# Loading x from two queues, and the modulation of the first two channel tiles summed by TensorE from the raw weights

## The chip, the cores and the metric

The kernel runs on one core of one Trainium2 chip. The metric is the device time of one execution in microseconds (us); the time of a version is the median over its runs. TensorE multiplies matrices, VectorE and ScalarE work elementwise, GpSimd does a few small operations, and SyncE issues nearly all DMAs. ScalarE issues some small ones.

## The reference, cut to what matters

One layer of a streaming encoder on `x` (512 x 1024) with a conditioning vector `c` (1024). What matters here is its beginning:

```python
cond = silu(c)
mod = cond @ w_ada + b_ada                 # w_ada: 1024 x 6144
sh1, sc1, g1, sh2, sc2, g2 = split(mod, 6)
u = layer_norm(x) * (1 + sc1) + sh1        # shift and scale per channel
z = u @ w_in                               # 1024 x 8192
```

Then two mixers (a gated recurrence and a spatial gating), their projections, a merge, `w_out`, a layer norm with `g1`, and a SwiGLU feed-forward layer with `sh2`, `sc2` and `g2`. All is in 32-bit floats.

## The kernel before

Channels lie on the partitions in eight tiles of 128 (`k` = 0 to 7), the 512 rows of x in the free dimension. To keep precision, each operand of a large product is split into a high part in a rounded format (`whi`, `uh`) and the rest (`wlo`, `ul`), and three products are summed: `whi*uh`, `wlo*uh`, `whi*ul`.

The part that the change touches is the head, the first 58 us. There:

- `x` comes in four row tiles (`load_x`), all on SyncE's queue. VectorE and GpSimd take each one's statistics, ScalarE normalises it (`x_norm`, L319), and TensorE transposes it channel tile by channel tile (`x_transpose`, L408).
- The small parameters come by ScalarE's queue: `c` into `cond`, and four pieces into the rows of `prow` (L282 to L285). TensorE's first instruction transposes `prow` (L451); ScalarE and GpSimd then make `bmod` from it, the bias of the modulation.
- `ada_cols(k, ...)` makes shift and scale for the two channel tiles k and k+1. It loads 1024 rows of `w_ada` for 256 shift and 256 scale columns in four DMAs of 512 KB. `step(d)` adds row tile d, weighted by `cond`, into the accumulator `adaacc` on VectorE (L346, L344); ScalarE can take a step (L342, into `prod`). `fin` sums the accumulator over the partitions: TensorE multiplies it with a matrix of ones (L363), and VectorE adds the bias (L365).
- `modulate(k)` (L412 to L414) applies shift and scale to the transposed tile: ScalarE makes `uf` and `uh`, VectorE `ul`.
- `lead(k, w, half)` (L420 to L423) multiplies channel tile k with the first 768 columns of the `u` section of `w_in`, in two halves of three column tiles, nine matmuls each. The six accumulators stay in PSUM over all eight channel tiles.
- `warm(n)` issues n products of ones (L401), each of which is two instructions in the profile, as is every 32-bit product here that isn't in the rounded format.

On TensorE, VectorE, ScalarE, GpSimd and SyncE this part runs in the order in which the code is written (`manual_schedule`). In the loop `for p in range(KT // 2)`, each turn has four `lead` calls, two `x_transpose` calls and one `fin`; VectorE works on the sums for the next two channel tiles (`steps`), on `split_part` of the next weight block, and on `modulate`. After the head, everything follows in one long stream on TensorE to the end.

Of the kernel before, what the change touches and what calls it, by code (L numbers as in the profile page):

```python
# [7 lines left out]
F32 = mybir.dt.float32  # L8
# [3 lines left out]
OP = mybir.AluOpType  # L12
# [3 lines left out]
P = 128  # L16
T = 512
NT = T // P
D = 1024
# [12 lines left out]
def f32(ap):  # L32
    return ap.bitcast(F32)
# [17 lines left out]
def body(ctx, tc, x, c, w_ada, b_ada, w_in, b_gate, lb_logits, norm_w, w_proj_a, g_ln_w, g_ln_b,  # L51
         g_ws, g_bs, w_proj_b, w_out, ln1_w, ln1_b, w_ffn_in, w_ffn_out, ln2_w, ln2_b, out):
    nc = tc.nc
    x, out = x[0], out[0]
    w_ada, b_ada, w_in, b_gate, norm_w = w_ada[0], b_ada[0], w_in[0], b_gate[0], norm_w[0]
# [4 lines left out]
    V, A, G, PE = nc.vector, nc.scalar, nc.gpsimd, nc.tensor  # L60
# [5 lines left out]
    ua = ctx.enter_context(tc.tile_pool(name="ua", bufs=12))  # L66
# [8 lines left out]
    def acc_ps():  # L75
        return acc.tile([P, 512], F32, name="acc")

    def side_ps():
        return side.tile([P, 512], F32, name="sps")

    def s2(name="s2"):
        return tmp["s2"].tile([P, 512], F32, name=name, tag="s2")
# [117 lines left out]
    blocks = []  # L200
# [59 lines left out]
    ident = cst.tile([P, P], F32, name="ident")  # L260
# [6 lines left out]
    mhalf = cst.tile([P, 4], F32, name="mhalf")  # L267
    V.memset(mhalf, -0.5)
    cond = cst.tile([P, 8], F32, name="cond")
    nc.scalar.dma_start(cond, c[0].rearrange("(a p) -> p a", p=P))  # L270
    A.activation(cond, cond, AF.Silu)
    par = cst.tile([P, P], F32, name="par")
    bmod = cst.tile([P, 8, 2], F32, name="bmod")
    bmod2 = cst.tile([P, 8, 2], F32, name="bmod2")
    mod1 = cst.tile([P, 8, 2], F32, name="mod1")
# [7 lines left out]
    nc.scalar.dma_start(prow[R_BG:R_BG + 16, :], b_gate.rearrange("g (a b) -> (g a) b", b=P))  # L283
    nc.scalar.dma_start(prow[R_LB:R_LB + 16, :], lb_logits.rearrange("g (a b) -> (g a) b", b=P))
    nc.scalar.dma_start(prow[R_NW:R_NW + 1, :], norm_w.rearrange("(a b) -> a b", b=P))  # L285
    xt = [ua.tile([P, 2, D], F32, name=f"x{i}", tag="u") for i in range(2)]

    def xtile(tt):
        return xt[tt // 2][:, tt % 2, :]

    def load_x(tts):
        for tt in tts:
            nc.sync.dma_start(xtile(tt), x[tt * P:(tt + 1) * P, :])

    load_x((0, 1))


    def ln_stats(xa):
        st = sm.tile([P, 2, 6], F32, name="bst")
# [18 lines left out]
    def normalise(dst, src, rn):  # L318
        A.activation(dst, src, AF.Identity, bias=rn[:, 1:2], scale=rn[:, 0:1])  # L319
# [33 lines left out]
    def ada_cols(k, m, b, s0, run=True):  # L353

        src = w_ada[:, s0 * D:(s0 + 2) * D].rearrange("r (s c) -> r s c", s=2)[:, :, k * P:(k + 2) * P]
        a, step = ada_acc(src, run)

        def fin(parts=None, b=b, js=(0, 1)):
            ps = side_ps().rearrange("p (o c) -> p o c", c=P)
            parts = parts or [a]  # L360
            for o, (j, i) in enumerate((j, i) for j in js for i in range(2)):
                for n, s in enumerate(parts):
                    PE.matmul(ps[:, o, :], s[:, i * 256 + j * P:i * 256 + (j + 1) * P], ones, start=n == 0, stop=n == len(parts) - 1)  # L363
            ks = slice(k + js[0], k + js[-1] + 1)
            V.tensor_tensor(m[:, ks, :], ps[:, 0:2 * len(js), 0].rearrange("p (k s) -> p k s", s=2), b[:, ks, :], OP.add)  # L365
        return fin if run else (fin, step)

    def ada_row(s0, q, g):

# [26 lines left out]
    tps = {}  # L396

    def warm(n):

        for _ in range(n):  # L400
            PE.matmul(lacc[NL - 1][:, 0:P], ones, ones, start=True, stop=True)  # L401

    def x_transpose(k, idle=()):
        tps[k] = side_ps()
        for tt in range(NT):
            if idle:
                warm(idle[tt])
            PE.transpose(tps[k][:, tt * P:(tt + 1) * P], xtile(tt)[:, k * P:(k + 1) * P], ident)  # L408

    def modulate(k):  # L410
        uf = s2("uf")
        A.activation(uf, tps[k], AF.Identity, bias=mod1[:, k, 0:1], scale=mod1[:, k, 1:2])  # L412
        A.activation(uh[k], uf, AF.Copy)
        V.tensor_tensor(ul[k], uf, f32(uh[k]), OP.subtract)  # L414

    def lead(k, w, half):
        js = [(lacc[j], slice(j * P, (j + 1) * P)) for j in range(half * NL // 2, (half + 1) * NL // 2)]
        wh, wl = w[0][:, k % 2, :], w[1][:, k % 2, :]
        for ps, cl in js:
            PE.matmul(ps, wh[:, cl], uh[k], start=k == 0, stop=False)  # L420
            PE.matmul(ps, wl[:, cl], uh[k], start=False, stop=False)
        for ps, cl in js:
            PE.matmul(ps, wh[:, cl], ul[k], start=False, stop=k == KT - 1)  # L423

    with tc.manual_schedule(engines={mybir.EngineType.DVE, mybir.EngineType.Activation, mybir.EngineType.Pool}):
        sts, mvs, rns = {}, {}, {}

        def x_stats(tt):
            sts[tt] = sm.tile([P, 2, 6], F32, name="bst")
            mvs[tt] = sm.tile([P, 2], F32, name="mv")  # L430
            rns[tt] = sm.tile([P, 2], F32, name="rn")
            for i in range(2):
                V.bn_stats(sts[tt][:, i, :], xtile(tt)[:, i * 512:(i + 1) * 512])
            V.bn_aggr(mvs[tt], sts[tt])
            V.tensor_scalar(rns[tt][:, 0:1], mvs[tt][:, 1:2], LN_EPS, None, op0=OP.add)
            V.tensor_scalar(rns[tt][:, 1:2], mvs[tt][:, 0:1], -1.0, None, op0=OP.mult)
            G.tensor_tensor(rns[tt][:, 0:1], rns[tt][:, 0:1], mhalf[:, 0:1], OP.pow)
            G.tensor_tensor(rns[tt][:, 1:2], rns[tt][:, 1:2], rns[tt][:, 0:1], OP.mult)

        def x_norm(tt):  # L440
            normalise(xtile(tt), xtile(tt), rns[tt])

        load_x((2, 3))
        ada = [ada_cols(0, mod1, bmod, 0, False)]
        blocks[0].load(1)
        for i in range(1, 3):
            ada.append(ada_cols(2 * i, mod1, bmod, 0, False))
            if i < 2:
                blocks[i].load()
        pps = side_ps()  # L450
        PE.transpose(pps[:, 0:P], prow, ident)  # L451
        for tt in range(NT):
            x_stats(tt)
            x_norm(tt)
            if tt == 1:
                A.activation(par, pps[:, 0:P], AF.Copy)
        for b, s0 in ((bmod, 0), (bmod2, 3)):
            G.tensor_copy(b[:, :, 0], par[:, R_ADA + 8 * s0:R_ADA + 8 * s0 + 8])
            G.tensor_scalar(b[:, :, 1], par[:, R_ADA + 8 * s0 + 8:R_ADA + 8 * s0 + 16], 1.0, None, op0=OP.add)
        G.tensor_scalar(hbg[:, 0:16], par[:, R_BG:R_BG + 16], 0.5, None, op0=OP.mult)  # L460
        G.tensor_scalar(hbg[:, 16:17], par[:, R_NW:R_NW + 1], 0.5, None, op0=OP.mult)

        def steps(p, k0, k1):
            for k in range(k0, k1):
                ada[p][1](k)

        fin, step = ada[0]
        prod = [s2("prod") for _ in range(2)]
        for k in range(8):
            step(k, prod[k - 6] if k >= 6 else None)  # L470
        blocks[0].split_part(0, 1)
        blocks[0].split_part(1, 1, G)
        x_transpose(0, (8, 6, 2, 2))
        fin(prod, js=(0,))
        fin(None, mod1, (0,))
        modulate(0)
        steps(1, 0, 2)
        fin(prod, js=(1,))
        fin(None, mod1, (1,))
        x_transpose(1)  # L480
        steps(1, 2, 4)
        modulate(1)
        for p in range(KT // 2):
            k, w, nxt = 2 * p, blocks[p].hl, blocks[p + 1]
            more = k + 2 < KT
            blocks[p + 2].load()
            if p == 0:
                ada.append(ada_cols(6, mod1, bmod, 0, False))
            lead(k, w, 0)
            if more:  # L490
                x_transpose(k + 2)
            if k:
                if more:
                    steps(p + 1, 2, 4)
                modulate(k + 1)
            lead(k, w, 1)
            if more:
                steps(p + 1, 4, 8)
            if more:
                nxt.split_part(0, 1)  # L500
            else:
                nxt.split()
            lead(k + 1, w, 0)
            if more:
                ada[p + 1][0]()
                if p + 2 < KT // 2:
                    steps(p + 2, 0, 2)
                modulate(k + 2)
            lead(k + 1, w, 1)
            if more:  # L510
                nxt.split_part(1, 1)
                x_transpose(k + 3)
        bpos[0] = KT // 2
# [372 lines left out]
    w = None  # L886
    for i in range(3 * NH):
        h = i // 3
        if i % 2 == 0:
            w = get()  # L890
        ps = acc_ps()
# [142 lines left out]
    for tt in range(NT):  # L1034
        ht = h1t(tt)
        bst = sm.tile([P, 2, 6], F32, name="bst")
        for hf in range(2):
            first = hf == 0 and tt < 2
            ps = head[tt] if first else acc_ps()
# [60 lines left out]
    part = {}  # L1100
# [134 lines left out]
    for hf in range(2):  # L1235
# [4 lines left out]
        ps = [acc_ps() for _ in range(NT)]  # L1240
        nb = len(KB) - 2
        fin = None
        for i, (k0, n) in enumerate(KB[:nb]):
            w = get()
            if hf == 0:
# [3 lines left out]
                fin = ada_row(5, i - 1, gate2) if i in (1, 2) else None  # L1249
# [37 lines left out]
```

## Time and profile before

| | us |
|---|---|
| median of 3 runs (lowest, highest) | 921.38 (921.32, 922.06) |
| the profiled execution | 921.51 |
| its span, first to last instruction | 919.7 |
| TensorE busy | 894.5 (97%) |
| VectorE busy | 727.4 (79%) |
| ScalarE busy | 412.1 (45%) |

The span is counted from the first instruction; 1.81 us of the profiled execution lie outside it. Times in the rows below are from the span's start. PE is TensorE's matmul stream, PEld its weight loads, DVE is VectorE, ACT is ScalarE, POOL is GpSimd, SP is SyncE; SPq and ACTq are their instruction queues, where DMAs are issued.

### The profile page before, as it was taken

What the parts mean: (1) busy time and instruction counts of PE and PEld (TensorE: products, weight loads), DVE (VectorE), ACT (ScalarE), POOL (GpSimd) and SP (SyncE); (2) the same over time, 40 slices, a digit from 0 to 9 for tenths busy, and PEclk for the clock granted to TensorE, in tenths of its full rate; (3) what the DMA queues carried; (4) which work ended last, traced back from release to release, by engine and by line L of the source; (5) the groups of instructions that cost most, each with busy time, mean ns of one, the idle gap of its engine ahead of it and who ended that gap; (6) DMA issues with size and microseconds to landing.
All of it is one profiled execution on the core that took longest, in us unless ns stands there. A gap on an engine that the chain in (4) does not pass through costs nothing.

```text
span 919.7 us, 12746 instructions
## 1 busy us (share of the span) xinstructions
PE 894.5 (97%) x5165; PEld 782.7 (85%) x5165; DVE 727.4 (79%) x1042; ACT 412.1 (45%) x542; POOL 132.3 (14%) x93
## 2 busy tenths in 40 slices
PE   5999999999999999999999999999999999999995
PEld 4888878888888888888888888999999999888884
DVE  5889977897878788885499879978888888964337
ACT  4465523234466666663233336644444445522110
POOL 2000010100000000000000012026555454000001
PEclk9999999999999999999999999999999999999998
DMA  9872432631533132231496614024432222742312
GB/s 307 289 242 101 127 103 92 236 130 46 138 92 92 47 91 73 66 92 46 149 348 244 212 55 138 1 93 132 133 102 92 93 92 96 272 142 87 115 46 91
DMA packets 105772, 118.30 MB, mean 129 GB/s; under 512 B 3617, under 2 KB 85618, under 8 KB 105714
## 3 DMA queue, kind: packets, MB, share of 16 engines
q1 hardware_dynamic: 104544, 117.45, 39.4%
q8 instruction: 40, 0.66, 0.3%
q10 hardware_dynamic: 1170, 0.05, 0.1%
q14 instruction: 18, 0.15, 0.0%
HBM read 115.39 MB, written 2.10 MB: 128 GB/s over the span
## 4 chain that ended last, share of the span: by engine, by line
PE 83%; DVE 10%; DMA 2%; POOL 2%; ACT 1%; issue 1%; POOLq 0%; DVEq 0%; ACTq 0%; SPq 0%
PE acc L1095 16%; PE acc L219 15%; PE acc L217 15%; PE acc L218 15%; PE sps L1095 7%; PE acc L601 5%; PE sps L601 2%; POOL rn L309 2%; PE sps L820 1%; DMA ada<-in_w_ada_dram 1%; PE sps L363 1%; DVE h L316 1%; PE sps L864 1%; PE sps L670 1%; PE sps L855 1%
## 5 line engine op out<-in xcount | busy, mean ns | idle before, releaser
L1095 PE MATMUL acc<-left,prod 128*128 128x256 f32 x1296 | 159.9, 283 | 1.4 <-DVE left L384 1.0
L1095 PEld LDWEIGHTS acc<-left,prod 128*128 128x128 f32 x1296 | 157.3, 192 | 1.9 <-DVE left L384 1.2
L149 ACT ACTIVATE whi<-raw 128x1024 fp32r<-128x1024 f32 (+2 forms) x92 | 91.0, 1016 | 135.0 <-PE acc L219 67.5
L150 DVE TENSOR_TENSOR wlo<-raw,whi 128x1024 fp32r<-128x1024 f32 (+2 forms) x91 | 105.5, 1174 | 45.3 <-ACT whi L149 39.9
L217 PE MATMUL acc<-uh,whi 128*128 128x512 f32 x336 | 134.7, 401 | 0.0
L219 PE MATMUL acc<-uh,wlo 128*128 128x512 f32 x336 | 131.4, 391 | 1.2 <-DVE wlo L150 1.2
L218 PE MATMUL acc<-ul,whi 128*128 128x512 f32 x336 | 131.0, 390 | 0.0
L219 PEld LDWEIGHTS acc<-uh,wlo 128*128 128x128 f32 x336 | 63.1, 188 | 15.1 <-DVE wlo L150 1.6
L1095 PE MATMUL sps<-left,prod 128*128 128x256 f32 x576 | 73.3, 283 | 0.5 <-DVE prod L384 0.5
L218 PEld LDWEIGHTS acc<-ul,whi 128*128 128x128 f32 x336 | 63.3, 188 | 12.0
L217 PEld LDWEIGHTS acc<-uh,whi 128*128 128x128 f32 x336 | 63.2, 188 | 11.8
L1095 PEld LDWEIGHTS sps<-left,prod 128*128 128x128 f32 x576 | 70.9, 192 | 0.7 <-DVE prod L384 0.7
L309 POOL TENSOR_TENSOR rn<-rn,mhalf 128x1 f32<-128x1 f32 x16 | 19.7, 1229 | 360.1 <-DVE rn L308 360.1
L384 DVE TENSOR_TENSOR prod<-raw,prod 128x1024 fp32r<-128x1024 f32 x42 | 55.0, 1308 | 19.2 <-ACT prod L383 19.1
L218 PE MATMUL acc<-wlo,hs 128*128 128x512 f32 x176 | 68.5, 389 | 0.0
L217 PE MATMUL acc<-whi,hs 128*128 128x512 f32 x176 | 68.5, 389 | 0.0
L219 PE MATMUL acc<-whi,hs 128*128 128x512 f32 x176 | 68.5, 389 | 0.0
L344 DVE SCALAR_TENSOR_TENSOR adaacc<-ada,cond,adaacc 128x512 f32<-128x512 f32 x82 | 61.5, 750 | 2.3 <-DMA ada<-in_w_ada_dram 0.7
L383 ACT ACTIVATE prod<-raw 128x1024 fp32r<-128x1024 f32 x42 | 44.5, 1059 | 40.3 <-PE acc L1095 21.4
L384 DVE TENSOR_TENSOR prod<-rawu,prod 128x1024 fp32r<-128x1024 f32 x22 | 47.8, 2171 | 8.3 <-ACT prod L383 7.7
L873 POOL TENSOR_TENSOR ss<-ss,mhalf 128x4 f32<-128x4 f32 x8 | 8.1, 1014 | 268.4 <-DVE ss L872 268.4
L219 PEld LDWEIGHTS acc<-whi,hs 128*128 128x128 f32 x176 | 33.0, 188 | 7.0
(293 smaller groups left out, 1763.9 us busy)
## 6 DMA issues: line engine op xcount, KB each, us to landing
ada<-in_w_ada_dram SPq DMA_DIRECT2D x32, 512.0 KB, 9.1
raw<-in_w_in_dram SPq DMA_DIRECT2D x13, 1024.0 KB, 5.8
raw<-in_w_in_dram SPq DMA_DIRECT2D x24, 512.0 KB, 5.5
raw<-in_w_ffn_in_dram SPq DMA_DIRECT2D x11, 1024.0 KB, 5.2
rawu<-in_w_ffn_in_dram SPq DMA_DIRECT2D x11, 1024.0 KB, 8.1
raw<-in_w_ffn_out_dram SPq DMA_DIRECT2D x10, 1024.0 KB, 5.2
ada<-in_w_ada_dram SPq DMA_DIRECT2D x8, 1024.0 KB, 7.7
rawq<-in_w_in_dram SPq DMA_DIRECT2D x4, 1024.0 KB, 8.7
```

The costliest lines, as they stand in the source:

```text
L149: A.activation(hi[:, k:k + n, :], self.raw[:, k:k + n, :], AF.Copy)
L150: eng.tensor_tensor(lo[:, k:k + n, :], self.raw[:, k:k + n, :], f32(hi[:, k:k + n, :]), OP.subtract)
L217: PE.matmul(ps, ah, bh, start=start, stop=False)
L218: PE.matmul(ps, ah, bl, start=False, stop=False)
L219: PE.matmul(ps, al, bh, start=False, stop=stop)
L309: G.tensor_tensor(rn[:, 0:1], rn[:, 0:1], mhalf[:, 0:1], OP.pow)
L316: V.scalar_tensor_tensor(xa, xa, rn[:, 0:1], wb[:, 1, :], op0=OP.mult, op1=OP.add)
L344: V.scalar_tensor_tensor(a, r, cond[:, k:k + 1], a, op0=OP.mult, op1=OP.add)
L383: A.activation(hi, src, AF.Copy)
L384: V.tensor_tensor(lo, src, f32(hi), OP.subtract)
L601: PE.matmul(o, a[:, k, s], b[:, k, :], start=n in (1, 5, 6) and k == 0 and a is ah and b is w[0], stop=n in (2, 4, 3) and k == 3 and a is ...
L1095: PE.matmul(ps[:, i, :], w[:, wi, k, cl], a[:, ai, k, :], start=first and st == (0, 0, 0, 0), stop=last and st == (1, 3, 0, 1), skip_group ...
```

## The change

1. `x` is allocated and loaded before the small parameters. Row tiles 0 and 2 go by SyncE's queue, 1 and 3 by ScalarE's, ahead of `cond` and `prow`.
2. The first two channel tiles get their shift and scale by `ada_col(k)`, each from four DMAs of 256 KB (rows of 128 columns), 1 MB for each tile. VectorE and ScalarE don't weight these rows any more: TensorE takes the raw weights as its stationary operand and `cond`, broadcast along the free dimension, as the moving one, and sums over all 1024 rows in PSUM (`part(0)` and `part(1)`, eight products each). One addition on VectorE gives the result.
3. In the issue order of the loads, the first weight block stands between `ada_col(0)` and `ada_col(1)`.
4. `x_transpose(0)` is taken apart (`x_one`), with 8 and 4 `warm` products in place of 8, 6, 2 and 2, and the two parts of tile 0 between the transposes.
5. The first half of `lead(0)` moves ahead of `part(1)` of channel tile 1. The split of the first block's second row tile moves from GpSimd to VectorE, behind it. `modulate(1)` now stands before `steps(1, 2, 4)`.

```diff
+    for tt in range(NT):
+        (nc.sync, nc.scalar)[tt % 2].dma_start(xtile(tt), x[tt * P:(tt + 1) * P, :])
     nc.scalar.dma_start(cond, c[0].rearrange("(a p) -> p a", p=P))
...
-    load_x((0, 1))
...
+    def ada_col(k):
+
+        r = ua.tile([P, 8, 2, P], F32, name="adac", tag="u")
+        for h in range(2):
+            for i in range(2):
+                nc.sync.dma_start(r[:, 4 * h:4 * h + 4, i, :],
+                                  w_ada[512 * h:512 * h + 512, i * D + k * P:i * D + (k + 1) * P].rearrange("(k p) c -> p k c", p=P))
+        ps = []
+
+        def part(h):
+            if not ps:
+                ps.append(side_ps())
+            for d in range(4 * h, 4 * h + 4):
+                for i in range(2):
+                    PE.matmul(ps[0][:, i * P:(i + 1) * P], r[:, d, i, :], cond[:, d:d + 1].to_broadcast([P, P]),
+                              start=(d, i) == (0, 0), stop=(d, i) == (7, 1), skip_group_check=True)
+
+        def fin():
+            V.tensor_tensor(mod1[:, k, :], ps[0].rearrange("p (o c) -> p o c", c=P)[:, 0:2, 0], bmod[:, k, :], OP.add)
+        return part, fin
...
-        load_x((2, 3))
-        ada = [ada_cols(0, mod1, bmod, 0, False)]
+        single = [ada_col(0)]
         blocks[0].load(1)
+        single.append(ada_col(1))
+        ada = [None]
...
-        fin, step = ada[0]
-        prod = [s2("prod") for _ in range(2)]
-        for k in range(8):
-            step(k, prod[k - 6] if k >= 6 else None)
+        tps[0] = side_ps()
+
+        def x_one(k, tt):
+            PE.transpose(tps[k][:, tt * P:(tt + 1) * P], xtile(tt)[:, k * P:(k + 1) * P], ident)
+
+        warm(8)
+        x_one(0, 0)
+        warm(4)
+        x_one(0, 1)
+        single[0][0](0)
+        x_one(0, 2)
+        single[0][0](1)
+        x_one(0, 3)
+        single[0][1]()
         blocks[0].split_part(0, 1)
-        blocks[0].split_part(1, 1, G)
-        x_transpose(0, (8, 6, 2, 2))
-        fin(prod, js=(0,))
-        fin(None, mod1, (0,))
         modulate(0)
         steps(1, 0, 2)
-        fin(prod, js=(1,))
-        fin(None, mod1, (1,))
+        single[1][0](0)
         x_transpose(1)
+        lead(0, blocks[0].hl, 0)
+        single[1][0](1)
+        blocks[0].split_part(1, 1)
+        single[1][1]()
+        modulate(1)
         steps(1, 2, 4)
-        modulate(1)
         for p in range(KT // 2):
...
-            lead(k, w, 0)
+            if k:
+                lead(k, w, 0)
```

## Rows read from the trace of the kernel before

**Rows 1.** The page: busy time, share of the span, instructions of TensorE.
```profile
PE 894.5 (97%) x5165; PEld 782.7 (85%) x5165; DVE 727.4 (79%) x1042; ACT 412.1 (45%) x542; POOL 132.3 (14%) x93
```
**Rows 2.** The chain that ended last, 0 to 45 us: start, length, what.
```profile
1.85 5.78 DMA prow<-in_b_gate_dram
...
8.06 9.18 DMA ada<-in_w_ada_dram
...
17.34 1.34 ACT prod L342 x2
...
29.44 0.76 DVE adaacc L344
```
**Rows 3.** TensorE in order of time, 8 to 24 us: start, length, instructions.
```profile
8.23 0.44 PE L451 MATMUL sps<-ident,prow 128*128 128x128 f32 x1 [8.23 <-DVE mv L434]
8.47 3.62 PE L401 MATMUL sps<-ones 128*128 128x128 f32 x16
...
12.10 1.55 PE L401 MATMUL sps<-ones 128*128 128x128 f32 x12
...
20.78 1.85 PE L363 MATMUL sps<-ones,prod 128*128 128x128 f32 x8
22.91 0.60 PE L408 MATMUL sps<-ident,x 128*128 128x128 f32 x4
23.27 0.48 PE L420 MATMUL acc<-uh,whi 128*128 128x512 f32 x1
```
**Rows 4.** Stages: busy per engine (instructions), granted clock PEclk, DMA share, GB/s.
```profile
0.00:8.20 8.20, 0.00 (x0) 0.00 (x0) 3.74 (x12) 2.52 (x3) 1.43 (x8) 1.00 0.78 233
8.20:12.20 4.00, 3.97 (x19) 4.00 (x20) 2.71 (x10) 2.78 (x4) 1.49 (x4) 1.00 0.98 314
...
15.60:18.10 2.50, 0.02 (x1) 0.00 (x0) 2.39 (x4) 0.76 (x2) 0.00 (x0) 1.00 1.04 379
18.10:23.30 5.20, 5.06 (x29) 4.88 (x29) 2.57 (x7) 3.44 (x5) 1.84 (x1) 0.67 1.10 352
...
33.70:43.70 10.00, 10.00 (x54) 8.41 (x53) 8.73 (x14) 4.36 (x7) 0.00 (x0) 1.00 0.81 273
```
**Rows 5.** VectorE in order of time, 17 to 34.8 us.
```profile
24.74 0.16 DVE L365 TENSOR_TENSOR mod<-sps,mod 128x2 f32<-128x2 f32 x1
24.82 1.53 DVE L344 SCALAR_TENSOR_TENSOR adaacc<-ada,cond,adaacc 128x512 f32<-128x512 f32 x2
26.47 0.69 DVE L414 TENSOR_TENSOR ul<-uf,uh 128x512 fp32r<-128x512 f32 x1
27.08 3.11 DVE L344 SCALAR_TENSOR_TENSOR adaacc<-ada,cond,adaacc 128x512 f32<-128x512 f32 x4
30.11 0.95 DVE L150 TENSOR_TENSOR wlo<-raw,whi 128x768 fp32r<-128x768 f32 x1
```
**Rows 6.** TensorE in order of time, 30.2 to 36.3 us.
```profile
30.34 1.13 PE L363 MATMUL sps<-ones,adaacc 128*128 128x128 f32 x8 [0.18 <-DVE adaacc L344]
31.22 0.48 PE L420 MATMUL acc<-uh,whi 128*128 128x512 f32 x1
...
33.39 0.60 PE L408 MATMUL sps<-ident,x 128*128 128x128 f32 x4
33.75 0.48 PE L420 MATMUL acc<-uh,whi 128*128 128x512 f32 x1
```
**Rows 7.** ScalarE and its DMA queue in order of time, 0 to 34.8 us.
```profile
0.71 0.47 ACTq L270 DMA_DIRECT2D cond<-in_c_dram  x1
...
5.59 0.21 ACT L271 ACTIVATE cond<-cond 128x8 f32<-128x8 f32 x1 [0.82 <-DMA cond<-in_c_dram]
```
**Rows 8.** Waits of SyncE's queue, 0 to 60 us: total, times, longest.
```profile
SPq L293 <- DMA cond<-in_c_dram: 3.5, 1, 3.5
```
**Rows 9.** DMA issues, 300 to 480 us: count, KB each, median us to landing.
```profile
raw<-in_w_in_dram SPq DMA_DIRECT2D x10, 512.0 KB, 5.5
raw<-in_w_in_dram SPq DMA_DIRECT2D x4, 1024.0 KB, 5.8
```

More of the change, by code (lines that the diff above doesn't have):

```diff
@@ L269, in body, with xtile @@
     cond = cst.tile([P, 8], F32, name="cond")
+    xt = [ua.tile([P, 2, D], F32, name=f"x{i}", tag="u") for i in range(2)]
+    def xtile(tt):
+        return xt[tt // 2][:, tt % 2, :]
+    for tt in range(NT):
+        (nc.sync, nc.scalar)[tt % 2].dma_start(xtile(tt), x[tt * P:(tt + 1) * P, :])
     nc.scalar.dma_start(cond, c[0].rearrange("(a p) -> p a", p=P))
@@ L285, in body @@
     nc.scalar.dma_start(prow[R_NW:R_NW + 1, :], norm_w.rearrange("(a b) -> a b", b=P))
[L286 to L293, printed above, removed]
-    load_x((0, 1))
     def ln_stats(xa):
```

## The prediction

> **What bounds the kernel now.** I read the page first: TensorE is busy for 97% of the span [rows 1]. What is to be had lies almost only in the head, before the long stream begins, so I followed the chain of waits from the start. It runs from the small parameters (`prow`) through a `w_ada` load that lands at 17.24 us, two weighted rows on ScalarE, and then through VectorE's sums for channel tiles 2 and 3, which end at 30.20 [rows 2]. In TensorE's own order the reader is to see that it starts when `prow` is there, at 8.23, runs products of ones, and makes its first product of `lead` at 23.27 [rows 3]. In the stages, TensorE has 2.5 us idle between 15.6 and 18.1, and from 33.7 on it is busy for every us of a turn of 10 us [rows 4]. From that point the kernel is TensorE's stream; whatever moves the first product of `lead(2)`, at 33.75 [rows 6], moves the end by as much. The last thing before it that TensorE waits for is the `fin` of channel tiles 2 and 3 at 30.34, which VectorE releases [rows 6]. So I cost the change by the time of that `fin`, since what follows it (8 instructions, nine products, four transposes) is unchanged.
>
> **What is removed.** The first `fin`s need 1 MB less of `w_ada` ahead of them, so the landing at 17.24 and ScalarE's 1.34 us behind it leave the path [rows 2]. Does the data still bind? The four x tiles are 2.10 MB, `ada_col(0)` 1.05 MB. At 233 GB/s over the first 8.2 us, 1.91 MB had moved, and the next stage ran at 314 GB/s [rows 4]; 3.15 MB are through at 8.2 + 1.24/0.314 = 12.1 us. Even two us of landing on top leave it at about 14. TensorE wants the second part of it at about 17 (below), so this load is hidden. Its pieces are 512 B in place of 1 KB; the case's blocks with such pieces land in 5.5 us for 512 KB, beside 5.8 us for 1 MB in 1 KB pieces [rows 9]. By the fixed part of those, anything from nothing to a doubling of its 3.3 us is possible; at the doubled price it lands at 15.4 to 17.4, just at the point of need. I take it as hidden. `ada_col(1)` and tiles 2 and 3 stand behind the same bytes as before, and are wanted later than before.
>
> **What TensorE gets.** A product of the unrounded kind is two instructions, at 0.11 us each (8 from 30.34 to 31.22 [rows 6]) at the full clock and at 0.23 us (16 in 3.62, 8 in 1.85) at the lower one [rows 3]. Each `part` is eight products, 16 instructions; four parts are 64, or 7.1 us. Away go 24 of the old `fin` and 12 of the warming. Call P the time at which TensorE starts. The transpose of `prow`, 16 warming instructions and the first transpose of x took 12.10 - 8.23 = 3.87 us [rows 3]; this beginning is the same. Then come 8 warming instructions and three parts (both of tile 0, the first of tile 1), 56 x 0.111 = 6.22 us, three single transposes of 0.09 and four more in 23.27 - 22.91 = 0.36 [rows 3]. I add 0.3 for VectorE's addition, whose PSUM bank the next sums take over (an estimate from its 0.16 us in rows 5 and the hand-overs around it). `lead(0)` starts at P + 3.87 + 6.22 + 0.27 + 0.36 + 0.3 = P + 11.0. Its `uh` is ready before that, since `uf` and `uh` run beside the first part of tile 1.
>
> Then nine products, 33.39 - 31.22 = 2.17 us [rows 6], and the second part of tile 1, 1.78 us and 0.15 to drain: shift and scale of tile 1 are summed at P + 15.1.
>
> **Where VectorE is late next.** Its order is now: addition for tile 1, `ul` of tile 1, then six weighted rows of tiles 2 and 3. Before, two of those stood ahead of `ul`. From the addition to the end of `ul` took 26.47 + 0.69 - 24.74 = 2.42 us, the six rows 1.53 + 3.11 = 4.64 [rows 5]. With 0.15 to hand over, the `fin` of tiles 2 and 3 can start at P + 15.1 + 2.42 + 4.64 + 0.15 = P + 22.3. TensorE, however, has only the transposes of tile 2 and two halves of `lead` in between (0.36 + 2 x 2.17) and is free for it at P + 11.0 + 2.17 + 1.78 + 0.36 + 4.34 = P + 19.65. It waits 2.65 us for VectorE. The split that comes from GpSimd costs VectorE about 0.95 us [rows 5], but in the time in which it waits for tile 1's sums, so nothing; without that cover the path would get these 0.95 us.
>
> So the gain of the earlier data is spent twice: on 7.1 us of products that VectorE and ScalarE did under the wait for data, and on six rows that now queue behind tile 1. The shift of the end is P + 22.3 - 30.34 = P - 8.0.
>
> **When TensorE starts.** P is 8.23 now. `prow` is behind `cond` in ScalarE's queue, and `cond` is its first issue at 0.71 and landed at 5.59 [rows 7], the piece `b_gate` at 7.63 [rows 2]. Now two x tiles are issued ahead of both. The same 2.10 MB then lie before `prow`, where the fourth tile had not been issued until `cond` landed (SyncE waited 3.5 us for that [rows 8]). Half a MB more at 314 GB/s is 1.7 us [rows 4], which gives P = 9.9. The bounds: nothing lost, 8.23; or x through at 8.2 + 0.19/0.314 = 8.8 and then the whole train from `cond` to TensorE's start, 8.23 - 5.59 = 2.64 us [rows 3, 7], 11.4. I take 9.9, near their middle, and get P - 8.0 = +1.9 us.
>
> The x tiles themselves come no sooner than the bytes allow: the DMA engines had a share of 0.78 of the first 8.2 us, with the ramp at the start in it, and 0.98 in the next stage [rows 4]. The Trainium skill says the same as a rule ("DMA: Bandwidth & Descriptors", section "Issuing engines are not separate DMA queues"): transfers issued from different engines share 16 DMA engines and interleave, and a second queue saves issue time only. By it the two queues bring no bandwidth, and small loads queued behind x on ScalarE wait for it; P is then late, as in my sum, and the rows' shares agree. If a second queue did bring bandwidth, x and `prow` would be sooner, P about 8.2, and the sum +0.2.
>
> **The rivals.**
> *Parameters no later.* If the small loads pass x on the way, P stays at 8.23 and the shift is +0.2 us, 921.7. For it: they landed in between x tiles before. Against it: they now stand behind x in their own queue. 0.17.
> *VectorE is not late.* If tiles 2 and 3 are summed by the time TensorE asks, the wait of 2.65 us is gone and the end shifts by P - 10.65: -0.8 at P = 9.9, and -2.4 at 8.23, some 919.1. It decides if the six rows lie beside TensorE's work; the order of VectorE's instructions speaks against it, the seven us less of VectorE and ScalarE work in the head for it. Any P under 10.65 makes it a gain. 0.12, with 0.10 over 0.2%.
> *The clock falls.* TensorE stood idle for 2.5 us before 18.1, and the granted clock then fell to the lower level for a part of 18.1 to 23.3 (mean 0.67 [rows 4]); 5.2 x 2 x 0.33 = 3.4 us at half rate, 1.7 us lost. The new wait of 2.65 us is as long, but follows dense work, where the old one followed a stretch with gaps. If it falls: +1.9 + 1.7 = +3.6, 925.1. 0.13.
>
> **How the numbers follow.** The sum, on the profiled execution's 921.51 (span 919.7; 0.13 above the median of 921.38): 921.5 + 1.9 = 923.4, with 0.58. Its own range, from P = 8.9 to 11.4 and half a us either way for when the clock rises at the start, is 922.0 to 925.4. What tells a change from none is 0.2%, 1.84 us, and the forecast lies just on that line: of its 0.58 I give 0.40 to slower. Slower: 0.40 + 0.13 = 0.53. Within: 0.18 + 0.17 + 0.02 = 0.37. Faster: 0.10. The range leaves out the best of the second rival and the worst of the third: 920.4 to 925.5.
>
> **What would show it.** Right: `prow`'s transpose on TensorE at 9 to 11 us; the `lead` of tile 0 about 11 us later, at about 21, so two us sooner than 23.27; TensorE waiting some 2.6 us for `adaacc` before the `fin` of tiles 2 and 3, at about 32.2; the first product of `lead(2)` at about 35.7 in place of 33.75; and unchanged turns of 10 us behind it. Wrong: no wait for `adaacc` there; a wait of TensorE for `adac` or of a `part` for DMA; a `part` that takes other than 1.8 us at the full clock (the broadcast moving operand is in no row); TensorE's start before 8.5; or later turns longer than 10 us.

## The result, and the profile after

The changed kernel took 925.93 us (median of four runs, 925.37 to 927.83), the kernel before 921.43 us (921.32 to 922.06) beside it: a ratio of 1.0052 (95% interval [1.004, 1.0064]; intervals stand in such brackets below). So it is slower, by more than the 0.2% that can be told from no change, and 0.4 us beyond the upper end of the forecast range. The profiled execution took 926.30 us with a span of 924.5, so 4.8 us more than the one of before.

The page, TensorE (answers to [rows 1]): 28 instructions more, which are the 64 new ones less 24 of the old `fin` and 12 of the warming, and 1.2 us more of work. That isn't 4.8, so most of the loss is waiting.

```profile
PE 895.7 (97%) x5193; PEld 784.4 (85%) x5193; DVE 723.6 (78%) x1035; ACT 410.4 (44%) x540; POOL 130.4 (14%) x92
```

TensorE in order of time in the kernel after (answers to [rows 3, 6]; the columns are start, length, line, instruction, and in brackets the idle time before it with what ended it):

```profile
12.20 0.45 PE L469 MATMUL sps<-ident,prow 128*128 128x128 f32 x1 [12.20 <-DVE bst L450]
...
17.49 1.95 PE L378 MATMUL sps<-cond,adac 128*128 128x128 f32 x16
...
23.43 0.48 PE L437 MATMUL acc<-uh,whi 128*128 128x512 f32 x1
...
34.57 1.16 PE L359 MATMUL sps<-ones,adaacc 128*128 128x128 f32 x8 [2.49 <-DVE adaacc L340]
...
37.98 0.48 PE L437 MATMUL acc<-uh,whi 128*128 128x512 f32 x1
```

TensorE starts at P = 12.20, 3.97 us later than before and 2.3 us later than forecast. From there on the forecast's sum holds: `lead(0)` at P + 11.2 (forecast 11.0), the `fin` of tiles 2 and 3 at P + 22.4 (forecast 22.3), with a wait of 2.49 us for VectorE (forecast 2.65). The first product of `lead(2)` is at 37.98 in place of 33.75 [rows 6]: 4.23 of the 4.8 us are lost by then.

VectorE in order of time, 24.5 to 34.5 us (answers to [rows 5]): the six rows of tiles 2 and 3 stand behind `ul` of tile 1, as forecast.

```profile
24.55 0.49 DVE L342 TENSOR_SCALAR adaacc<-ada,cond 128x512 f32<-128x512 f32 x1 [0.68 <-DMA ada<-in_w_ada_dram]
...
25.74 0.95 DVE L150 TENSOR_TENSOR wlo<-raw,whi 128x768 fp32r<-128x768 f32 x1
27.55 0.16 DVE L382 TENSOR_TENSOR mod<-sps,bmod 128x2 f32<-128x2 f32 x1 [0.86 <-PE sps L378]
29.22 0.69 DVE L431 TENSOR_TENSOR ul<-uf,uh 128x512 fp32r<-128x512 f32 x1 [1.51 <-ACT uh L430]
29.83 4.68 DVE L340 SCALAR_TENSOR_TENSOR adaacc<-ada,cond,adaacc 128x512 f32<-128x512 f32 x6
```

The chain of waits ends the same way (answers to [rows 2]): `ul` of tile 1, the six rows, the `fin`. But it leads its first 12 us through x and VectorE's statistics (`bst`), as the first line of TensorE above does. TensorE's transpose of `prow` reads neither, so the name in that place is only the event that came last before it; what it really waits for is in the loads.

ScalarE and its DMA queue (answers to [rows 7]). Two things are new. `cond` is used at 11.21 (before 5.59). And there are gaps in the issuing: from 6.66 to 8.21 the queue has nothing ahead of `norm_w`'s load and still doesn't issue it.

```profile
0.72 0.89 ACTq L276 DMA_DIRECT2D x<-in_x_dram  x2
1.64 0.46 ACTq L277 DMA_DIRECT2D cond<-in_c_dram  x1
2.13 2.82 ACTq L289 DMA_DIRECT2D prow<-in_b_ada_dram  x1
5.86 0.32 ACTq L290 DMA_DIRECT2D prow<-in_b_gate_dram  x1
6.21 0.45 ACTq L291 DMA_DIRECT2D prow<-in_hgrn_lb_logits_dram  x1
8.21 0.46 ACTq L292 DMA_DIRECT2D prow<-in_hgrn_norm_w_dram  x1
...
11.21 0.21 ACT L278 ACTIVATE cond<-cond 128x8 f32<-128x8 f32 x1 [1.22 <-DMA cond<-in_c_dram]
```

Waits of SyncE's queue (answers to [rows 8]; the columns are total, times, longest). Loads of `adac` wait for x and for `cond`, with which they share no data:

```profile
SPq L369 <- DMA x<-in_x_dram: 5.5, 1, 5.5
SPq L369 <- DMA cond<-in_c_dram: 2.3, 1, 2.3
```

The semaphores in the trace tell why: the loads take eight completion semaphores in turn, whichever queue they are on, so a load is not issued until the one eight places ahead has landed. `norm_w` is issued at 8.21, 0.02 us after the x tile that had its semaphore. With four x tiles placed ahead, three of the four loads into `prow` come up against an x tile.

The time from issue to landing (KB each, median us) shows what TensorE's start waits for:

```profile
prow<-in_b_ada_dram ACTq DMA_DIRECT2D x1, 24.0 KB, 9.3
cond<-in_c_dram ACTq DMA_DIRECT2D x1, 4.0 KB, 9.6
prow<-in_b_gate_dram ACTq DMA_DIRECT2D x1, 8.0 KB, 5.8
prow<-in_hgrn_lb_logits_dram ACTq DMA_DIRECT2D x1, 8.0 KB, 5.6
```

By these semaphores `cond` landed at 11.19, 2.66 us after the last x tile ahead of it in its queue (8.53). The loads into `prow` landed right behind it, at 11.44, 11.64, 11.85 and 11.89, though the first was issued at 2.13 and the last, `norm_w`, at 8.21; TensorE starts 0.31 us later. So the order in the queue and the held issue end within 0.04 us of each other, and `norm_w`'s late issue is not by itself what made the start late. In the kernel with the six rows left out (below) `norm_w`, issued at 8.16, landed at 11.34, ahead of the two loads before it.

`cond` is 1024 pieces of 4 bytes. From 8.0 to 9.5 us ScalarE's queue (q10) moved them almost one for one with the 512 B pieces of `adac` in SyncE's (q1); the columns are packets, MB and the share of the 16 DMA engines:

```profile
q1 hardware_dynamic: 736, 0.37, 93.5%
q10 hardware_dynamic: 738, 0.00, 32.0%
```

Stages (answers to [rows 4]; busy time by engine, granted clock, DMA share, GB/s). More moves in the first 8.2 us, 272 GB/s for 233. From 8.2 to 12.2 it is 175 GB/s for 314: up to 11.2 the DMA engines are full, but of small pieces, and in the last us they have nothing to do, since SyncE's next load waited until 11.21 for `cond`. Between 23.3 and 33.7 TensorE is idle for 1.6 us and from 33.7 on for 0.9, both in the wait for `adaacc`. The granted clock is at its upper level in all of them.

```profile
0.00:8.20 8.20, 0.00 (x0) 0.00 (x0) 3.03 (x11) 0.00 (x0) 1.35 (x8) 1.00 0.77 272
8.20:12.20 4.00, 0.00 (x1) 0.04 (x2) 3.83 (x12) 2.27 (x3) 1.58 (x5) 1.00 0.88 175
...
8.20:11.20 3.00, 0.00 (x0) 0.00 (x0) 2.86 (x10) 1.28 (x1) 1.21 (x4) 1.00 1.17 233
11.20:12.20 1.00, 0.00 (x1) 0.04 (x2) 0.96 (x3) 0.99 (x2) 0.37 (x2) 1.00 0.01 1
...
23.30:33.70 10.40, 8.78 (x51) 7.32 (x49) 7.17 (x11) 2.84 (x4) 0.00 (x0) 1.00 1.07 361
33.70:43.70 10.00, 9.13 (x48) 7.74 (x49) 9.04 (x15) 4.30 (x6) 0.00 (x0) 1.00 1.04 357
```

### The profile page after: what moved, and what is told of

Read it like the earlier page. It is cut to its first block, busy times and chain, and to the rows that moved or that the text cites. A ratio compares the mean times of both kernels' runs of the same rounds, so it can differ in the third digit from the quotient of the medians.

```text
span 924.5 us, 12788 instructions
## 1 busy us (share of the span) xinstructions
PE 895.7 (97%) x5193; PEld 784.4 (85%) x5193; DVE 723.6 (78%) x1035; ACT 410.4 (44%) x540; POOL 130.4 (14%) x92
## 3 DMA queue, kind: packets, MB, share of 16 engines
q10 hardware_dynamic: 1458, 1.09, 0.4%
## 4 chain that ended last, share of the span: by engine, by line
PE 84%; DVE 10%; POOL 2%; DMA 1%; ACT 1%; issue 1%; POOLq 0%; DVEq 0%; ACTq 0%
PE acc L1123 16%; PE acc L219 15%; PE acc L218 15%; PE acc L217 15%; PE sps L1123 7%; PE acc L629 5%; PE sps L629 2%; POOL rn L305 2%; PE sps L848 1%; DVE h L312 1%; PE sps L378 1%; PE sps L892 1%; PE sps L698 1%; PE sps L883 1%; PE sps L359 1%
## 5 line engine op out<-in xcount | busy, mean ns | idle before, releaser
L340 DVE SCALAR_TENSOR_TENSOR adaacc<-ada,cond,adaacc 128x512 f32<-128x512 f32 x77 | 57.7, 749 | 2.2 <-DMA ada<-in_w_ada_dram 0.7
```

The lines of the kernel that those rows point to most:

```text
L340: V.scalar_tensor_tensor(a, r, cond[:, k:k + 1], a, op0=OP.mult, op1=OP.add)
```

## The experiments

The theories: the loss is TensorE's late start, since the small loads stand behind x; or it is VectorE's order, with six rows behind tile 1; or the new products on TensorE themselves. Each kernel changes the one after, but for the first below, which changes the one before. The kernel before ran beside each at 921.43 to 921.49 us.

**The x part alone.** The kernel before, with x loaded as in the change:

```diff
+    for tt in range(NT):
+        (nc.sync, nc.scalar)[tt % 2].dma_start(xtile(tt), x[tt * P:(tt + 1) * P, :])
     nc.scalar.dma_start(cond, c[0].rearrange("(a p) -> p a", p=P))
...
-    load_x((0, 1))
...
-        load_x((2, 3))
```

> The kernel before with the x part alone: x allocated and loaded first, tiles 1 and 3 on ScalarE's queue ahead of cond and prow; modulation by VectorE as before. Theory A: TensorE starts late as in the changed kernel (P about 12.2), but here it has 36 products of ones and idle time of 2.5 us to absorb it; lead(0) at about 22 to 24, the fin of tiles 2 and 3 between 29.5 and 31.5, time 920.5 to 922.5. Rival D (the x part alone costs the 4 us, whatever follows): 925 or more. If x from two queues were a gain in bandwidth that reaches the path: below 919.5.

Measured: 921.36 us, ratio 1.0001 [0.9992, 1.001]. TensorE in this kernel, its start and the `fin` of tiles 2 and 3:

```profile
12.73 0.45 PE L446 MATMUL sps<-ident,prow 128*128 128x128 f32 x1 [12.73 <-DVE rn L432]
...
30.40 1.13 PE L359 MATMUL sps<-ones,adaacc 128*128 128x128 f32 x8 [0.73 <-DVE adaacc L340]
```

It starts even later than in the kernel after, by 4.5 us against before, and the `fin` is 0.06 us later than before. The old head had so much waiting for data between its products [rows 3, 4] that a late start disappears in it. Loading x from two queues costs nothing by itself here; it costs with a head in which TensorE works without a gap from its start on.

**The small loads written first.** The x loop is moved behind the loads of the parameters:

```diff
-    for tt in range(NT):
-        (nc.sync, nc.scalar)[tt % 2].dma_start(xtile(tt), x[tt * P:(tt + 1) * P, :])
     nc.scalar.dma_start(cond, c[0].rearrange("(a p) -> p a", p=P))
...
     nc.scalar.dma_start(prow[R_NW:R_NW + 1, :], norm_w.rearrange("(a b) -> a b", b=P))
+    for tt in range(NT):
+        (nc.sync, nc.scalar)[tt % 2].dma_start(xtile(tt), x[tt * P:(tt + 1) * P, :])
```

> The changed kernel with cond and the four prow loads issued on ScalarE's queue ahead of x tiles 1 and 3; all else as changed. Theory A (small loads wait behind x in their queue and then crawl beside the w_ada pieces; TensorE's start P sets everything, the fin of tiles 2 and 3 comes at P + 22.4): P falls from 12.20 to about 8.2, fin to about 30.6, the time to about 921.8 (4 us less than the changed kernel, level with before). Rival B (the 512-byte w_ada pieces are late by themselves): P falls, but TensorE then waits for adac, fin at 32 or later, time 923.5 or more. Rival C (the sums on TensorE cost the time wherever it starts): time stays at 925 to 926.

Measured: 925.51 us, ratio 1.0053 [1.004, 1.0066], so no gain. ScalarE's queue shows that the edit didn't do what it says: the scheduler issued an x tile second, `b_gate` stands behind the activation of `cond`, which waited for `cond` to land, and `norm_w` waited for an x tile as before. The last two lines are from issue to landing.

```profile
0.72 0.49 ACTq L275 DMA_DIRECT2D cond<-in_c_dram  x1
1.24 0.60 ACTq L292 DMA_DIRECT2D x<-in_x_dram  x1
1.87 0.44 ACTq L287 DMA_DIRECT2D prow<-in_b_ada_dram  x1
...
5.63 0.21 ACT L276 ACTIVATE cond<-cond 128x8 f32<-128x8 f32 x1 [2.00 <-DMA cond<-in_c_dram]
5.63 0.33 ACTq L288 DMA_DIRECT2D prow<-in_b_gate_dram  x1
...
8.40 0.46 ACTq L290 DMA_DIRECT2D prow<-in_hgrn_norm_w_dram  x1
...
prow<-in_b_ada_dram ACTq DMA_DIRECT2D x1, 24.0 KB, 6.7
prow<-in_b_gate_dram ACTq DMA_DIRECT2D x1, 8.0 KB, 5.5
```

TensorE started at 12.01, and its `fin` came at 33.90 = P + 21.9. So this says nothing against the late start. It shows that late issues alone can bring it: with `cond` out of the way `b_ada`, issued at 1.87, landed at 8.6, but `b_gate`, issued at 5.63, only at 11.1, and `norm_w` at 11.65. It shows too that `cond`, now first in its queue, was there at 5.63, with two x tiles moving in the other queue; it is x ahead of it in its own queue that kept it to 11.21.

**c loaded as rows of `prow`.** The 4-byte pieces of `cond` could be what makes the small loads slow. Here c comes as eight rows of 512 B, one more load into `prow`, and is transposed with it (the `Silu` of `mhalf` only keeps the table's load where it was):

```diff
-    nc.scalar.dma_start(cond, c[0].rearrange("(a p) -> p a", p=P))
-    A.activation(cond, cond, AF.Silu)
+    A.activation(cond[:, 0:4], mhalf, AF.Silu)
...
+    nc.scalar.dma_start(prow[96:104, :], c[0].rearrange("(a b) -> a b", b=P))
...
+                A.activation(cond, par[:, 96:104], AF.Silu)
```

> The changed kernel with c loaded as eight rows of 512 bytes into prow, in place of 1024 pieces of 4 bytes into cond; cond is taken from the transposed prow, with a small activation at the start so that the table is there. x still stands ahead of it. Theory A with the 4-byte pieces as the cause: x is through at about 7.7 us, then some 90 rows remain, P about 9.2 to 9.7, fin at about 31.8, time about 923. Rival F (the place behind x is the cause, the pieces are not): P at 11 or later, time 925 or more.

Measured: 929.38 us, ratio 1.0087 [1.0074, 1.0101]. The added load took its turn among the semaphores: it was held for a load of `adac` and issued at 10.28, and TensorE starts 3.9 us behind it, at 14.22, though `bst` ended at 11.55 in this kernel. So it is `prow` that TensorE's start waits for, not x. The other theory, the pieces, isn't refuted by the time: with `cond` out of the queue `b_ada`, issued at 1.72 behind two x tiles, landed at 8.6 (6.9 us), 0.23 us behind the x tile, where in the kernel after it landed at 11.44. `cond` did hold up what stood behind it; the loads issued late then hid that. Whether its place or its 4-byte pieces did more is not separated. ScalarE's queue, then TensorE:

```profile
1.72 0.37 ACTq L288 DMA_DIRECT2D prow<-in_b_ada_dram  x1
...
10.28 0.28 ACTq L292 DMA_DIRECT2D prow<-in_c_dram  x1
```

```profile
14.22 0.44 PE L469 MATMUL sps<-ident,prow 128*128 128x128 f32 x1 [14.22 <-DMA raw<-in_w_in_dram]
...
36.76 2.08 PE L359 MATMUL sps<-ones,adaacc 128*128 128x128 f32 x8 [2.49 <-DVE adaacc L340]
```

The `fin` is again at P + 22.5. Its eight instructions take 2.08 us in place of 1.16: after the wait of 2.49 us the clock was at its lower level here (mean 0.53 over 36.3 to 39.9), which the same wait in the kernel after did not bring.

**The small loads issued first.** ScalarE's queue is put in its written order: `cond`, the four loads into `prow`, then its x tiles.

```diff
+    with tc.manual_schedule(engines={mybir.EngineType.Activation}):
+        nc.scalar.dma_start(cond, c[0].rearrange("(a p) -> p a", p=P))
...
+        nc.scalar.dma_start(prow[R_NW:R_NW + 1, :], norm_w.rearrange("(a b) -> a b", b=P))
+        for tt in range(NT):
+            (nc.sync, nc.scalar)[tt % 2].dma_start(xtile(tt), x[tt * P:(tt + 1) * P, :])
+        A.activation(cond, cond, AF.Silu)
```

> The changed kernel with ScalarE's queue in a written order: cond and the four prow loads, then x tiles 1 and 3, then the activation of cond. The trace of the run with the params first showed that they were not issued first: x tile 1 went ahead of b_ada, and the last prow load was issued at 8.4 us, when an earlier load had landed, and TensorE started 3.6 us behind it. Theory A2 (TensorE's start P is the issue of the last small load and 3.6 to 5.3 us; the fin of tiles 2 and 3 is at P + 22.4): the last prow load goes out at about 3 us, P is about 8.2, fin about 30.6, time about 921.7, level with before. Rival B (w_ada pieces late): a wait of TensorE for adac, fin at 32 or later, 923 or more. Rival C (the sums on TensorE cost 4 us wherever it starts): 925.

Measured: 925.56 us, ratio 1.0045 [1.0033, 1.0058]. The last small load is issued at 2.90 and TensorE starts at 7.38, 4.8 us earlier than in the kernel after. Yet the `fin` gains 1.9 us in the profiled execution (924.36 us), and the median next to nothing. VectorE and then TensorE in this kernel:

```profile
23.59 0.49 DVE L343 TENSOR_SCALAR adaacc<-ada,cond 128x512 f32<-128x512 f32 x1 [3.45 <-DMA ada<-in_w_ada_dram]
...
27.31 0.69 DVE L432 TENSOR_TENSOR ul<-uf,uh 128x512 fp32r<-128x512 f32 x1 [1.51 <-ACT uh L431]
27.92 4.69 DVE L341 SCALAR_TENSOR_TENSOR adaacc<-ada,cond,adaacc 128x512 f32<-128x512 f32 x6
```

```profile
7.38 0.45 PE L470 MATMUL sps<-ident,prow 128*128 128x128 f32 x1 [7.38 <-POOL rn L456]
...
32.66 1.16 PE L360 MATMUL sps<-ones,adaacc 128*128 128x128 f32 x8 [2.86 <-DVE adaacc L341]
```

A second bound takes over. VectorE is ready for tiles 2 and 3 at 20.1, their data come at 23.59, and its order from there (the first two rows, the split, tile 1's `mod` and `ul`, the six rows) takes 9.07 us. In this order of loads the data can't come much sooner: from 12.2 to 23.6 the DMA engines were full, with a share of 1.09 at 333 GB/s (in two kernels below they come 0.9 to 1.0 us earlier). With P at 12.20 this bound lies at 24.55 + 9.07 = 33.6, just below P + 22.4 = 34.6, so it hid behind the late start.

**VectorE's order.** The first two of the six rows ahead of tile 1's `ul`, as in the kernel before:

```diff
-        modulate(1)
         steps(1, 2, 4)
+        modulate(1)
```

> The changed kernel with modulate(1) and steps(1, 2, 4) exchanged, as they stood before: VectorE does two weighted rows of tiles 2 and 3 while ScalarE makes uf and uh of tile 1. Theory A: the wait of TensorE for adaacc shrinks by the two rows, 1.5 us, from 2.5 to about 1.0; fin at about 33.1, time about 924.4. Rival E (VectorE would be held by ul of tile 1 or by the data of tiles 2 and 3 all the same): no change, 925.9.

Measured: 924.60 us, ratio 1.0036 [1.0022, 1.005], 1.3 us less than after; TensorE's wait falls from 2.49 to 0.91.

```profile
32.67 1.16 PE L359 MATMUL sps<-ones,adaacc 128*128 128x128 f32 x8 [0.91 <-DVE adaacc L340]
```

**Both.** The small loads issued first and VectorE's order; then, beside both, the split of the second row tile given back to GpSimd:

```diff
+        blocks[0].split_part(1, 1, G)
         modulate(0)
...
-        blocks[0].split_part(1, 1)
         single[1][1]()
-        modulate(1)
         steps(1, 2, 4)
+        modulate(1)
```

> The run before (small loads first) and the exchange of modulate(1) and steps(1, 2, 4) together. Theory A2: the two are independent, so 1.5 us less than with the small loads first alone: fin at about 29.1, time about 920.2, 1.2 us less than the kernel before. Rival E (the data of tiles 2 and 3 hold VectorE then): as with the small loads first alone.

> The run with small loads first and the exchanged order, and beside it the split of the first block's second row tile back on GpSimd, right behind the first split, as before the change. In the traces with the small loads first, VectorE waits for the data of tiles 2 and 3 until 22.7 to 23.6 us, and then does two rows, the split (0.95 us), and the addition for tile 1 in this order. Theory A3 (two bounds, the later one holds: TensorE's start and the sums on TensorE; or the landing of tiles 2 and 3 and what VectorE has in its order behind it): the split's 0.95 us leave VectorE, the addition comes when TensorE's sums are ready, fin moves from 30.2 to about 29.4, time 0.7 us less than that run, 921.8, or 0.3 over to 0.7 under the kernel before. Rival G (no data bound: TensorE's own work sets it): no change.

Measured: 922.54 us without GpSimd, ratio 1.0014 [1.0005, 1.0023]; 922.32 us (920.78 to 924.01) with it, 1.0015 [1.0006, 1.0024]. Each step shortens the order behind the data: 9.07 us, then 22.68 to 30.17 = 7.49, then 22.58 to 29.34 = 6.76, 0.3 less than the kernel before has (23.29 to 30.34 [rows 6]). The last `fin`:

```profile
29.34 1.16 PE L360 MATMUL sps<-ones,adaacc 128*128 128x128 f32 x8 [0.91 <-DVE adaacc L341]
```

That is 1.0 us ahead of the kernel before, and the profiled execution is the shortest of its runs, 920.78 us. The median isn't: its 11 runs spread over 3.2 us. Why they do is open, since only one of them has a trace.

**All of x on one queue.** The small loads first, and all x tiles on SyncE, so that of the change only the new head is left:

```diff
-            (nc.sync, nc.scalar)[tt % 2].dma_start(xtile(tt), x[tt * P:(tt + 1) * P, :])
+            nc.sync.dma_start(xtile(tt), x[tt * P:(tt + 1) * P, :])
```

> The changed kernel with the x part undone: small loads first on ScalarE's queue, all four x tiles on SyncE's; only the sums on TensorE stay. Theory A2: P about 8.2, and the same time as with two queues and the small loads first, about 921.7; the second queue brings nothing that reaches the path. If two queues matter by bandwidth: 1 us or more slower than that run.

Measured: 925.75 us, ratio 1.0047 [1.0034, 1.0059], the same as with two queues (925.56). The Trainium skill has it as a rule ("DMA: Bandwidth & Descriptors", section "Issuing engines are not separate DMA queues") that loads from different engines share the same DMA engines and that a second one saves only the time to issue; this pair agrees. TensorE starts at 8.14, a place in which one of the forecast's rivals expected +0.2 us. The data for tiles 2 and 3 come at 23.21, and 9.07 us later:

```profile
32.28 2.08 PE L360 MATMUL sps<-ones,adaacc 128*128 128x128 f32 x8 [2.90 <-DVE adaacc L341]
...
37.28 0.48 PE L438 MATMUL acc<-uh,whi 128*128 128x512 f32 x1
```

```profile
32.20:35.70 3.50, 3.42 (x12) 3.13 (x13) 2.16 (x5) 1.07 (x2) 0.00 (x0) 0.51 1.06 376
```

Here the clock was at its lower level for about 3.4 us behind the wait, and from the `fin` to `lead(2)` it took 5.00 us where the kernel before took 33.75 - 30.34 = 3.41 [rows 6]: 1.6 us lost.

**The six rows left out.** In the kernel after, and in the one with the small loads issued first:

```diff
-                ada[p][1](k)
+                if p > 1 or k < 2:
+                    ada[p][1](k)
```

> The changed kernel without VectorE's weighted rows 2 to 7 of tiles 2 and 3 (left out of the computation, so shift and scale of these two tiles are sums over 256 of 1024 rows); TensorE's work is whole. Theory A3: the price of VectorE's lateness is read directly: TensorE's wait for adaacc of 2.5 us is gone, fin at about 32.0 with P at 12.2, time about 923.3, still 1.8 us slower than before: that part is the late start and the longer sums on TensorE. Rival G (VectorE isn't the gate, the wait is only named after it): 925 or more.

> The run with the small loads first, and the same six rows left out. Theory A3: both bounds are loosened; what stays is the landing of tiles 2 and 3 at about 23.6, behind which two rows, a split, the addition, and uf and uh of tile 1 stand before lead(1): fin at about 29.6, time about 922 (profile about 921.3). If instead TensorE's start were the only bound: fin at P + 19.65, about 27.2, time 919.

Measured: 922.94 us, ratio 1.0021 [1.0012, 1.003], and 921.21 us, ratio 1.0000 [0.9991, 1.0009]. TensorE in the first of them:

```profile
12.06 0.45 PE L469 MATMUL sps<-ident,prow 128*128 128x128 f32 x1 [12.06 <-DVE mv L451]
...
31.31 1.05 PE L359 MATMUL sps<-ones,adaacc 128*128 128x128 f32 x8
```

With no wait for VectorE the `fin` is at P + 19.25 (the forecast had TensorE free for it at P + 19.65). VectorE's lateness is worth 3.0 us of the 4.5. With the start early as well, at 7.44, TensorE doesn't wait for VectorE either, but it waits 0.9 us for `adac` and 0.6 for x, and the `fin` comes at 29.59 = P + 22.15; the kernel is even with the one before. So the sums on TensorE buy nothing here even with VectorE's six rows gone, and what is late then is the loads. Whether they would pay with those in time, at the forecast's P + 19.65, no run tells.

## Why the prediction was wrong

The direction, the place and the sum from TensorE's start on were right; the start itself was not. The loss is 4.5 us for a forecast of 1.9. (The sum's own range starts at 921.9 by its terms, not 922.0; nothing hangs on that.)

- **When TensorE starts: here it failed.** The step took the small loads as issued as before and late only by the bytes ahead of them, "half a MB more at 314 GB/s is 1.7 us", P = 9.9, with 11.4 as the worst. Measured: 12.20. The x tiles were through as the worst case had it, at 8.53 for 8.8. But `cond`, whose 4 KB count nothing by bytes, landed 2.66 us behind them, and the loads into `prow` behind `cond`, at 11.44 to 11.89. The worst case had `cond` there together with x and then 2.64 us to the start; the second part was 1.0. The step also took the issues as they were, while three of the four loads into `prow` were now issued only as x tiles landed. Each is enough for a start near 12: late issues alone gave 12.01, and behind `cond` even `b_ada`, issued at 2.13, landed at 11.44. With both gone TensorE started at 7.38 and 8.14. The last issue by itself doesn't tell the start: 3.6 to 5.3 us lie between the two in the kernels of this case. The case had shown a wait for an issue before: SyncE's fourth x tile waited 3.5 us for `cond` [rows 8]. The forecast quoted it and read it as a matter of x alone; it did not ask which load the same rule would hold next. This term gives 2.3 us of the miss. Its reason, x ahead in the queue, was right; its price by bytes was not.
- **One us of P is one us of the end.** True for the kernel after, P + 22.4, and false below a P of about 10: the data of tiles 2 and 3 plus VectorE's 9.07 us are a second bound. The statement that these data "are wanted later than before" holds only with the late start; with the early one they are wanted at 20.1 and late by 3.45 us. So the rival "parameters no later", at +0.2 us, was priced wrongly too: with P at 8.14 the `fin` was 1.9 us later than before, and the median 4.3 us.
- **VectorE late next.** Right: 2.49 us of waiting for a forecast 2.65, six rows in 4.68 us for 4.64, and the exchange of the order gave back 1.3 us.
- **The split from GpSimd hidden.** Right as put, with its condition: in the kernel after VectorE waits 0.86 us for tile 1 behind it. Where the cover is gone, it costs: taking it away again moved the `fin` by 0.83 us between the two kernels of "Both", 0.10 of it from the data.
- **The products.** Right: 16 instructions of a `part` at 1.79 us from start to start, with the broadcast operand, for a forecast of 1.78; 28 more instructions in all.
- **`adac` hidden.** Right with the late start, no wait in the kernel after. With the early one TensorE waited for it, 0.2 to 0.8 us at a time.
- **The clock.** It did not fall in the profiled execution of the kernel after, so this rival takes no part in its 4.8 us. Its price was right, 1.6 us for 1.7, where it came: in two other kernels, behind waits of 2.49 and 2.90 us, while it stayed up behind waits of 2.49 and 2.86 us in the kernel after and in the one with the small loads first. What decides between them is open, and so is its part in runs without a trace. One reading of the rows was loose: the 16 products that took 3.62 us at the start ran at half the rate, but the granted clock of their stretch is 1.00 [rows 4], so the profile doesn't show that slow start as a lower clock.
- **"Unchanged turns behind it".** Not quite. The kernel after loses a further 0.8 us at about 560 us, in a wait that the kernel before doesn't show in that place:

```profile
PE sps L1009 <- ACT un L315: 0.8, 1, 0.8
```

All ten kernels of the experiments have it as well, with 0.5 to 1.7 us, the one with the x part alone with 0.5. Its cause is open; no experiment was aimed at it.

## What to carry to other kernels

Before loads are moved forward, count pieces and loads in flight as well as bytes. A load of 4 KB in 4-byte pieces, put behind large loads in its queue, holds up all that stands behind it; and a small load can be held until a large one has landed, the sign of which is a gap in the issuing queue with nothing ahead of it. To see which of the two a start waits for, compare the landings, not the issues. Work moved from engines that wait for data to the engine that bounds the kernel is free only as long as that engine waits too; here TensorE's idle head was the cover that made the old sums cheap. And a step that waits on two chains gains nothing from the repair of one: compute the time of each chain (here P + 22.4, and data + 9.07) before choosing which to shorten.

## What the runs showed of the hardware

- The order of issue within one queue sets when a small load is there: `cond`, 4 KB, was in use at 5.63 with two x tiles in the other queue, and at 11.21 behind two x tiles in its own. The Trainium skill ("DMA: Bandwidth & Descriptors", section "Queues, rings and completion order") says that each issuing engine has its own ring on every DMA engine and that these are worked off in order; both times agree with it.
- Pieces count beside bytes: the 4-byte pieces of `cond` moved almost one for one with the 512 B pieces of the other queue (738 packets and 736 in 1.5 us), and the load landed 2.66 us behind x.
- An issue can wait for another load's landing: `norm_w`'s came at 8.21, 0.02 us after that of an x tile, where before it came at 2.93. The Trainium skill says, on the same page under "Anatomy of one DMA — SWDGE (gpsimd) path", that DMA engines do not wait for semaphores and that the issuing sequencer does. The section is on another way to issue, but ScalarE's and SyncE's queues behaved so here.
- A wait of the same length, 2.49 us, behind dense work was followed by the lower clock in one kernel (36.3 to 39.9 us, mean 0.53) and by the upper one in another (1.00 from 33.7 to 43.7).
